# Weight halves in one ring of seven 8 KB tiles, and plain weights split two pairs at a time

## The chip, the cores and the metric

The kernel runs on one core of a Trainium2 chip. The metric is device time in microseconds (us): the time from start to end of one execution, the median of several. Before the change it is 1951.76 us, the median of three runs from 1951.52 to 1951.91.

A core has five engines, each with its own instruction stream: PE (TensorE, matrix products), DVE (VectorE, elementwise), ACT (ScalarE, elementwise and casts), POOL (GpSimd) and SP (SyncE, which here only issues transfers). They meet through semaphores. Transfers between the chip's memory and SBUF run on 16 DMA engines, which the queues of SP, ACT and POOL feed.

## The reference

One decoder block on 256 tokens of width 2048, all in float32. In short:

```python
h = x
h = h + 0.5 * swiglu(rms_norm(h, ffn1_norm), ffn1_w_gu, ffn1_w_down)    # FFN 1, inner width 5632
h = h + hybrid_mixer(rms_norm(h, mix_norm), w_in, ..., w_out)           # gated DeltaNet and stick-breaking heads
h = h + 0.5 * swiglu(rms_norm(h, ffn2_norm), ffn2_w_gu, ffn2_w_down)    # FFN 2
h = h + sigmoid(rms_norm(h, ple_norm) @ ple_w_gate) * (p @ ple_w_proj)
out = rms_norm(h, final_norm)

def swiglu(x, w_gu, w_down):
    gate, up = split(x @ w_gu, 2)
    return (silu(gate) * up) @ w_down
```

Nearly all the arithmetic is in the weight products. The two FFNs hold about two thirds of them.

## The kernel before

**Halves.** A float32 product is made from operands in a shorter type. Each operand is split: hi is the value cast to that type, lo is the rest, and a product is hi·hi + hi·lo + lo·hi: three matmuls of 128x512. For weights ACT makes hi (a cast, L74) and DVE makes lo (a subtract, L75). A *pair* is two 128-row slices of a block of 512 columns: 512 KB in memory, 4 KB in each of the 128 partitions. It is loaded to a raw tile by SP's queue (L71), split, and used by PE in 12 matmuls: two slices, two halves of the tokens, three products. `weight_pair` (L64 to 76) does this. There are four raw tiles, and three tiles each for hi and lo.

**Seven products.** In the FFNs part of the inner dimension is done by a Strassen-like scheme that makes seven products of eight. The four quarters of such a piece of weights (R0 to R3, 1 MB each, tag R) are loaded, DVE adds them up step by step (L304, some adds are done by an accumulating DMA on POOL's queue, L311), and at seven points the sum that then stands in a quarter is split to hi and lo (L295 on ACT, L296 on DVE; 128x2048 elements for a gate/up operand, 128x1536 or 128x1024 for a down product). `all_sums` is a generator for these seven operands, s0 to s6, with two tiles each for hi and lo of 8 KB. On the activations' side `halves` (L420 and on) builds the sums S and their halves Sh and Sl: an add (L452), four adds on quarters of it (L458), a cast (L460) and a subtract (L461). A full operand is used in 12 matmuls, one of a down product in 9 or 6. Each of the first four products is also copied or subtracted between banks (L344, L347, L349).

**Groups.** An FFN is a list of groups: 11 of gate/up (gu0 to gu10), each making 512 columns of gate and of up, and 6 of the down product (dn), two after each of the three parts of the inner dimension (3, 4 and 4 gate/up groups). The first or the second of two down groups makes columns 0 to 1023 or 1024 to 2047. While a group's plain pairs run, the seven products of the *next* group run between them, one after each plain pair from the second or third on. FFN 1 begins with two gate/up groups without seven-product operands, FFN 2 with one. At the end of a gate/up group DVE multiplies silu(gate) with up (L477), transposes it (L482) and later splits it (L500); after a down group's block DVE adds the result to h (L551).

**The order of the weights.** `plan` writes the whole order down ahead: a list of pairs, sum operands and loads of quarters. `next_weights` (L82 to 97) is called by PE's side for each operand that it uses. It goes through the list and issues what it may: pairs as long as no more than LEAD = 2 are split ahead of use, sum operands as long as no more than one is ahead. The two kinds are counted apart. A load in the list is issued when it is reached: the first four quarters of an FFN by SP's queue, the later ones by POOL's.

A scheduler then orders each engine's instructions by its own estimates. It keeps dependencies, and it may put matmuls of the hi half ahead of those of an operand whose lo half it expects late.

## Time and profile before

| | us |
|---|---|
| median of three runs | 1951.76 |
| the profiled run's own time | 1953.25 |
| its span in the profile | 1951.5 |
| granted TensorE clock, mean | 0.998 |
| PE / DVE / ACT busy | 1932.7 / 1567.9 / 1163.1 |
| DMA mean | 243 GB/s |

How to read the profile. The page gives busy time by engine and the chain of work that ended last, followed back from the last instruction. A group line gives the source line, engine, operation, the tile written and the tiles read, the shape, the number of instructions, then busy us and the mean ns of one, and behind the second bar the engine's idle time just ahead of them and what ended it. A timeline row has the start and the duration in us, the same names, and in brackets the idle time before it and what ended that; "x4" means four in a row put together. A row of the windows has, after the window and its length, the busy us of PE, PEld (weight loads, beside PE), DVE, ACT and POOL with the numbers of instructions, the granted clock, the busy share of the DMA engines and GB/s. SPq is SP's transfer queue.

### The profile page before, as it was taken

To read this page: it belongs to the slowest core of one execution; us is meant where nothing else is said; L and a number is where in the kernel's file an instruction comes from. 1 tells how busy PE (TensorE), PEld (TensorE's weight loads), DVE (VectorE), ACT (ScalarE), POOL (GpSimd) and SP (SyncE) were. 2 spreads that over 40 slices of the span, in tenths; PEclk is the share of its full clock that TensorE was granted. 3 is DMA by queue.
4 is the path that set the end of the run, shared out by engine and by line. 5 is a ranking of instruction groups with operands and counts; after the bars stand their busy time and mean duration, and the time that the engine had idled before them with its cause. 6 is when DMAs were issued, how large, how long until landed. Compare 5 with 4: busy or idle time off the path is not lost.

```text
span 1951.5 us, 24163 instructions
## 1 busy us (share of the span) xinstructions
PE 1932.7 (99%) x8884; PEld 1591.6 (82%) x8884; DVE 1567.9 (80%) x1679; ACT 1163.1 (60%) x1358; POOL 148.8 (8%) x226
## 2 busy tenths in 40 slices
PE   9999999999999999999999999999999999999997
PEld 7888888888888888878788888888888788887886
DVE  7889878997889766797856579889888987888965
ACT  6656666566665567664555456566565755656653
POOL 0010100000010000010100000010000100001000
PEclk9999999999999999999999999999999999999999
DMA  8778888788887765556565786888898987988864
GB/s 311 268 238 276 255 288 285 227 293 251 282 283 237 225 216 172 175 169 209 173 201 160 244 289 226 226 285 289 241 282 251 303 266 237 272 255 282 249 208 141
DMA packets 144184, 475.06 MB, mean 243 GB/s; under 512 B 19649, under 2 KB 47297, under 8 KB 129857
## 3 DMA queue, kind: packets, MB, share of 16 engines
q1 hardware_dynamic: 107200, 302.16, 44.4%
q0 software_dynamic: 25920, 160.44, 30.2%
q10 hardware_dynamic: 10944, 10.91, 1.7%
q8 instruction: 69, 1.13, 0.2%
q14 instruction: 51, 0.41, 0.1%
HBM read 451.44 MB, written 22.02 MB: 243 GB/s over the span
## 4 chain that ended last, share of the span: by engine, by line
PE 87%; DVE 6%; DMA 4%; issue 2%; ACT 1%; SPq 0%; POOL 0%; POOLq 0%; DVEq 0%; ACTq 0%
PE g L340 5%; PE d L541 5%; PE d L542 5%; PE g L339 5%; PE d L540 4%; PE g L341 4%; PE u L540 4%; PE u L542 4%; PE u L541 4%; PE g L541 4%; PE g L542 4%; PE pj L109 4%; PE pj L110 4%; PE pj L111 4%; PE g L540 4%
## 5 line engine op out<-in xcount | busy, mean ns | idle before, releaser
L74 ACT CAST whi<-raw 128x1024 fp32r<-128x1024 f32 (+1 forms) x489 | 512.1, 1050 | 427.1 <-PE pj L111 109.9
L75 DVE TENSOR_TENSOR wlo<-raw,whi 128x1024 fp32r<-128x1024 f32 (+1 forms) x489 | 592.0, 1217 | 166.1 <-ACT whi L74 163.8
L296 DVE TENSOR_TENSOR slo<-R,shi 128x2048 fp32r<-128x2048 f32 (+2 forms) x224 | 445.2, 1989 | 149.0 <-ACT shi L295 147.6
L295 ACT CAST shi<-R 128x2048 fp32r<-128x2048 f32 (+2 forms) x224 | 374.2, 1671 | 140.5 <-DVE R L304 62.1
L109 PE MATMUL pj<-whi,nTh 128*128 128x512 f32 x448 | 179.4, 401 | 0.0
L110 PE MATMUL pj<-wlo,nTh 128*128 128x512 f32 x448 | 175.3, 391 | 1.1 <-DVE wlo L75 1.1
L111 PE MATMUL pj<-whi,nTl 128*128 128x512 f32 x448 | 174.9, 390 | 0.0
L541 PE MATMUL d<-wlo,hTh 128*128 128x512 f32 x448 | 174.3, 389 | 0.0
L540 PE MATMUL d<-whi,hTh 128*128 128x512 f32 x448 | 174.2, 389 | 0.0
L542 PE MATMUL d<-whi,hTl 128*128 128x512 f32 x448 | 173.7, 389 | 0.0
L541 PE MATMUL g<-wlo,nTh 128*128 128x512 f32 x400 | 155.9, 390 | 0.4 <-DVE wlo L75 0.4
L541 PE MATMUL u<-wlo,nTh 128*128 128x512 f32 x400 | 155.7, 389 | 0.5 <-DVE wlo L75 0.5
L542 PE MATMUL g<-whi,nTl 128*128 128x512 f32 x400 | 155.8, 390 | 0.0
L542 PE MATMUL u<-whi,nTl 128*128 128x512 f32 x400 | 155.7, 389 | 0.0
L540 PE MATMUL g<-whi,nTh 128*128 128x512 f32 x400 | 155.4, 390 | 0.0
L540 PE MATMUL u<-whi,nTh 128*128 128x512 f32 x400 | 154.2, 389 | 0.2 <-ACT whi L74 0.2
L304 DVE TENSOR_TENSOR R<-R 128x2048 f32<-128x2048 f32 (+2 forms) x68 | 135.7, 1995 | 0.1
L110 PEld LDWEIGHTS pj<-wlo,nTh 128*128 128x128 f32 x448 | 84.2, 188 | 18.9 <-DVE wlo L75 2.7
L111 PEld LDWEIGHTS pj<-whi,nTl 128*128 128x128 f32 x448 | 84.1, 188 | 17.6
L542 PEld LDWEIGHTS d<-whi,hTl 128*128 128x128 f32 x448 | 84.1, 188 | 17.6
L541 PEld LDWEIGHTS d<-wlo,hTh 128*128 128x128 f32 x448 | 84.1, 188 | 17.6
L540 PEld LDWEIGHTS d<-whi,hTh 128*128 128x128 f32 x448 | 84.1, 188 | 17.4
(332 smaller groups left out, 3445.2 us busy)
## 6 DMA issues: line engine op xcount, KB each, us to landing
raw<-in_w_gu SPq DMA_DIRECT2D x199, 512.0 KB, 5.7
raw<-in_w_down SPq DMA_DIRECT2D x112, 512.0 KB, 6.5
raw<-in_w_in SPq DMA_DIRECT2D x112, 512.0 KB, 3.4
R<-in_w_gu2q POOLq DMA_DIRECT2D x54, 1024.0 KB, 8.6
R<-in_w_gu1q POOLq DMA_DIRECT2D x48, 1024.0 KB, 8.6
raw<-in_w_out SPq DMA_DIRECT2D x32, 512.0 KB, 4.2
tT<-scr SPq DMA_DIRECT2D x22, 512.0 KB, 5.1
R<-in_w_down11q POOLq DMA_DIRECT2D x12, 768.0 KB, 6.0
```

Of the source, the lines that this page charges most:

```text
L74: nc.scalar.copy(hi[:, j, :], raw[:, j, :])
L75: nc.vector.tensor_tensor(out=lo[:, j, :], in0=raw[:, j, :], in1=hi[:, j, :], op=ALU.subtract)
L109: nc.tensor.matmul(outs[t], xh[:, c], whi[:, j, :], start=st, stop=False)
L110: nc.tensor.matmul(outs[t], xh[:, c], wlo[:, j, :], start=False, stop=False)
L111: nc.tensor.matmul(outs[t], xl[:, c], whi[:, j, :], start=False, stop=sp)
L295: keep(nc.scalar.copy(hi, w))
L296: nc.vector.tensor_tensor(out=lo, in0=w, in1=hi, op=ALU.subtract)
L304: keep(nc.vector.tensor_tensor(out=self.raw[x], in0=self.raw[x], in1=self.raw[y], op=ALU.add))
L339: nc.tensor.matmul(out, xh, whi[:, g, :], start=st, stop=False, skip_group_check=True)
L540: nc.tensor.matmul(out, xh[:, c], whi[:, j, :], start=st, stop=False, skip_group_check=True)
L541: nc.tensor.matmul(out, xh[:, c], wlo[:, j, :], start=False, stop=False, skip_group_check=True)
L542: nc.tensor.matmul(out, xl[:, c], whi[:, j, :], start=False, stop=sp, skip_group_check=True)
```

## The change

It has three parts.

- **Raw tiles**: two of 8 KB in place of four of 4 KB. Each holds two pairs, loaded by two transfers, and is free again when both are split (class `Pairs`).
- **One ring.** The tiles for hi and lo of plain pairs (six of 4 KB) and of sum operands (four of 8 KB) become seven tiles of 8 KB: three in the pool that lives through the program (w), four in the FFN's (f), taken in the order of RING. A single pair takes one w tile for both halves. A sum operand, or a quad, takes two tiles, one for hi and one for lo. An operation is issued as soon as its tiles' last users are done in the list and not over `ahead` operations wait; that number doesn't bind, the seven tiles do.
- **Quads.** In the FFNs two plain pairs that follow one another in the list (other than the first two of an FFN, and those of FFN 2's last group) are split together: one cast and one subtract of 128x2048 (`halved`, L69 to 71). The lines are L70 (cast) and L71 (subtract) for plain weights, L392 and L393 for sum operands, L380 for the adds of quarters, L91 for the raw loads, L361 for the quarters, L569 and L574 for L477 and L482, L544, L550, L552 and L553 for S, and L644 for L551. Sum operands are made by `next_operand`, called once for each.

The built program has 154 quads, and 181 subtracts on plain weights that are not of a quad. The number of matmuls and their operands are unchanged, and the bytes loaded too.

The core of the diff:

```diff
-LEAD = 2
+RING = "ffwfwfw"
+CAP = {x: RING.count(x) for x in "wf"}
...
-        raw = wp.tile([P, 2, NB], F32, tag="raw", name="raw", bufs=4)
-        hi = pool.tile([P, 2, NB], F32R, tag="whi", name="whi", bufs=bufs)
-        lo = pool.tile([P, 2, NB], F32R, tag="wlo", name="wlo", bufs=bufs)
...
+    def new_raw():
+        return wp.tile([P, 4, NB], F32, tag="raw", name="raw", bufs=2)
+
+    def halved(hi, lo, src):
+        nc.scalar.copy(hi, src)
+        nc.vector.tensor_tensor(out=lo, in0=src, in1=hi, op=ALU.subtract)
...
+        def load(self):
+            if self.raw is None:
+                self.raw = new_raw()
+                n = 2 if done[0] else 1
+                for k in range(0, 2 * len(self.srcs), n):
+                    nc.sync.dma_start(out=self.raw[:, k:k + n], in_=self.srcs[k // 2][:, k % 2:k % 2 + n])
+            return self.raw
...
+        def issue(self, where):
+            slots = [(wp if x == "w" else current[0]).tile([P, NS, NB], F32R, tag="w", name="w",
+                                                            bufs=CAP[x]) for x in where]
+            if self.kind == "sum":
+                self.out = [self.src.next_operand(*slots)]
+            elif self.kind == "single":
+                raw = self.src.load()[:, 2 * self.at:2 * self.at + 2]
+                self.out = [weight_pair(raw, slots[0], 2 if not done[0] else 1)]
+            else:
+                halved(slots[0], slots[1], self.src.load())
+                self.out = [tuple(x[:, 2 * i:2 * i + 2] for x in slots) for i in range(2)]
...
     def next_weights():
 
-        ahead = max(1, min(LEAD, done[1] // 2))
-        while done[0] < len(order):
-            kind, src = order[done[0]]
-            if kind != "load" and sum(k == kind for k, _ in split) > (ahead if kind == "pair" else 1):
-                break
+        ahead = max(1, done[1] // 2)
...
+            if any(len(ring[x]) + where.count(x) - CAP[x] > sum(not o.left for o in ring[x][:where.count(x)])
+                   for x in "wf"):
+                break
+            if sum(o.left > 0 for o in set(ring["w"] + ring["f"])) > ahead:
+                break
+            op.issue(where)
...
-                hi = fp.tile([P, NS, NB], F32R, tag="shi", name="shi", bufs=2)[:, 0:self.ns]
-                lo = fp.tile([P, NS, NB], F32R, tag="slo", name="slo", bufs=2)[:, 0:self.ns]
...
+        pairs = [i for i in range(first, behind_at.get(n, len(order))) if order[i][0] == "pair"][2:]
+        quads.update(pairs[:len(pairs) // 2 * 2])
```

Two places where the built programs differ. The first is SP's queue at the end of the mixer and the start of FFN 2 (in_w_gu20 and in_w_gu2q are its first gate/up weights, plain and in quarters). Before:

```order
L71 DMA raw_9544<-in_w_gu20 128x1024
L71 DMA raw_9566<-in_w_gu20 128x1024
L71 DMA raw_9624<-in_w_gu20 128x1024
L71 DMA raw_9652<-in_w_gu20 128x1024
L71 DMA raw_9686<-in_w_gu20 128x1024
L71 DMA raw_9704<-in_w_gu20 128x1024
L276 DMA R_9658<-in_w_gu2q 128x2048
L276 DMA R_9660<-in_w_gu2q 128x2048
L276 DMA R_9662<-in_w_gu2q 128x2048
L276 DMA R_9664<-in_w_gu2q 128x2048
L71 DMA raw_9722<-in_w_gu20 128x1024
L71 DMA raw_9740<-in_w_gu20 128x1024
```

SP's queue at the same place, now:

```order
L91 DMA raw_8932<-in_w_gu20 128x1024 x2
L91 DMA raw_9010<-in_w_gu20 128x1024 x2
L361 DMA R_9015<-in_w_gu2q 128x2048
L361 DMA R_9017<-in_w_gu2q 128x2048
L361 DMA R_9019<-in_w_gu2q 128x2048
L361 DMA R_9021<-in_w_gu2q 128x2048
L91 DMA raw_9047<-in_w_gu20 128x1024 x2
L91 DMA raw_9074<-in_w_gu20 128x1024 x2
```

The loads of the fifth and sixth pair, raw_9686 and raw_9704 before, stood ahead of the four quarters; now (raw_9047) they stand behind them, where they wait for the subtract of the second pair.

The second place is DVE in FFN 1, in the second down group of the first part, while the products of the next gate/up group begin between its pairs (slo and w<-R are the lo halves of that group's operands s1 and s2, S its activations' sum, d0 and d1 the down product's banks). Before:

```order
L458 TENSOR_TENSOR S_1563<-S_1563 128x2x128
L75 TENSOR_TENSOR wlo_1573<-raw_1571,whi_1572 128x1024
L458 TENSOR_TENSOR S_1563<-S_1563 128x2x128
L75 TENSOR_TENSOR wlo_1613<-raw_1611,whi_1612 128x1024
L458 TENSOR_TENSOR S_1563<-S_1563 128x2x128
L296 TENSOR_TENSOR slo_1607<-R_1387,shi_1606 128x2048
L461 TENSOR_TENSOR Sl_1531<-S_1563,Sh_1530 128x1024
L551 SCALAR_TENSOR_TENSOR h_89<-d0_1307,h_89 128x512
L551 SCALAR_TENSOR_TENSOR h_89<-d1_1308,h_89 128x512
L75 TENSOR_TENSOR wlo_1650<-raw_1648,whi_1649 128x1024
L75 TENSOR_TENSOR wlo_1689<-raw_1687,whi_1688 128x1024
L296 TENSOR_TENSOR slo_1645<-R_1420,shi_1644 128x2048
```

DVE at the same place, now:

```order
L71 TENSOR_TENSOR w_1379<-raw_1380,w_1378 128x2048
L393 TENSOR_TENSOR w_1392<-R_1275,w_1391 128x2048
L544 TENSOR_TENSOR S_1431<-nTh_100,nTl_104 128x1024
L380 TENSOR_TENSOR R_1275<-R_1275,R_1323 128x2048
L550 TENSOR_TENSOR S_1431<-S_1431 128x2x128 x4
L393 TENSOR_TENSOR w_1440<-R_1275,w_1439 128x2048
L553 TENSOR_TENSOR Sl_1410<-S_1431,Sh_1409 128x1024
L380 TENSOR_TENSOR R_1275<-R_1275,R_1335 128x2048
L644 SCALAR_TENSOR_TENSOR h_89<-d0_1195,h_89 128x512
L644 SCALAR_TENSOR_TENSOR h_89<-d1_1196,h_89 128x512
L71 TENSOR_TENSOR w_1488<-raw_1489,w_1487 128x2048
L393 TENSOR_TENSOR w_1495<-R_1275,w_1494 128x2048
```

The narrow subtracts wlo_1573 and wlo_1613 stood among the adds of S, ahead of Sl and of the updates of h. The wide subtract of the quad w_1487 stands behind the second add of quarters (L380) and behind both updates of h (L644), and between it and the wide subtract of w_1378 there are twelve other instructions.

More of the change, by code (lines that the diff above doesn't have):

```diff
@@ L69, in weight_pair @@
+    def weight_pair(raw, w, parts=1):
         for i in range(parts):
             j = slice(2 * i // parts, 2 * (i + 1) // parts)
[L71 to L80 removed]
@@ L82, in next_weights @@
[L82 to L95 removed]
+            halved(w[:, 0:2][:, j], w[:, 2:4][:, j], raw[:, j])
@@ L399, in plan @@
             todo = []
+            if group.kind == "behind":
+                behind_at[n] = len(order)
             for j, (b, g) in enumerate(group.plain):
```

129 lines of the change are left out of this document (93 added, 36 removed).

## The prediction

> **What bounds the kernel now.** First the page: the span, the engines' busy time and the chain that ended last.
>
> ```profile
> span 1951.5 us, 24163 instructions
> PE 1932.7 (99%) x8884; PEld 1591.6 (82%) x8884; DVE 1567.9 (80%) x1679; ACT 1163.1 (60%) x1358; POOL 148.8 (8%) x226
> PE 87%; DVE 6%; DMA 4%; issue 2%; ACT 1%; SPq 0%; POOL 0%; POOLq 0%; DVEq 0%; ACTq 0%
> ```
>
> PE bounds it. The change leaves PE its 8884 matmuls, so its time is moved only by how long PE waits for operands. DVE and ACT have idle time of their own; what they save counts only where PE waits. The windows give each stage (first FFN, then the second; after the window come us and PE's busy time and instructions):
>
> ```profile
> 0.00:646.00 646.00, 642.84 (x2816) 527.05 (x2816) 546.11 (x480) 397.15 (x398) 57.35 (x92) 1.00 0.84 269
> 1155.40:1906.00 750.60, 748.77 (x3294) 614.29 (x3294) 636.83 (x568) 459.99 (x469) 64.32 (x98) 1.00 0.83 260
> ```
>
> A matmul is recorded longer than the distance to the next one, so a short wait hides between two records. I therefore count starts, in PE's timeline at the start of the second FFN:
>
> ```profile
> 1159.13 0.39 PE L540 MATMUL g<-whi,nTh 128*128 128x512 f32 x1
> ...
> 1167.29 0.39 PE L540 MATMUL g<-whi,nTh 128*128 128x512 f32 x1
> 1167.52 0.39 PE L541 MATMUL g<-wlo,nTh 128*128 128x512 f32 x1
> ```
>
> The first two rows are three pairs apart, 36 matmuls in 8.16 us: 0.2267 us each, 2.72 for a pair of weights (12 matmuls) and 2.72 for a full seven-product operand. At that pace the first FFN's 2816 matmuls take 638.4 of 646.0 us and the second's 3294 take 746.7 of 750.6. All waiting of PE in both FFNs is 7.6 + 3.9 = 11.5 us; no better feeding gains more there. The clock is 1.00 in both.
>
> How near to waiting PE already is shows in DVE's timeline where the first FFN goes from a down product back to gate/up, and in PE's beside it:
>
> ```profile
> 184.00 1.22 DVE L452 TENSOR_TENSOR S<-nTh,nTl 128x1024 f32<-128x1024 f32 x1
> 185.13 2.28 DVE L296 TENSOR_TENSOR slo<-R,shi 128x2048 fp32r<-128x2048 f32 x1
> 187.33 0.42 DVE L458 TENSOR_TENSOR S<-S 128x256 f32<-128x256 f32 x1
> 187.67 2.28 DVE L304 TENSOR_TENSOR R<-R 128x2048 f32<-128x2048 f32 x1
> 189.87 0.42 DVE L458 TENSOR_TENSOR S<-S 128x256 f32<-128x256 f32 x1
> ...
> 195.35 1.22 DVE L461 TENSOR_TENSOR Sl<-S,Sh 128x1024 fp32r<-128x1024 f32 x1
> 196.49 1.28 DVE L551 SCALAR_TENSOR_TENSOR h<-d,h 128x512 f32<-128x512 f32 x2
> 197.69 2.35 DVE L75 TENSOR_TENSOR wlo<-raw,whi 128x1024 fp32r<-128x1024 f32 x2
> 200.33 2.29 DVE L296 TENSOR_TENSOR slo<-R,shi 128x2048 fp32r<-128x2048 f32 x1 [0.29 <-ACT shi L295]
> ```
>
> ```profile
> 202.46 0.39 PE L339 MATMUL g<-shi,Sh 128*128 128x512 f32 x1
> 202.68 0.49 PE L340 MATMUL g<-slo,Sh 128*128 128x512 f32 x1
> ```
>
> The last low half is done at 200.33 + 2.29 = 202.62, and PE takes it at 202.68, 0.06 us later, and loses about 0.1. The slack at this place is nil. Whatever reaches DVE later than now is paid by PE in full.
>
> **The change, part by part.** The groups by form price its instructions (mean ns behind the busy time):
>
> ```profile
> L75 DVE TENSOR_TENSOR wlo<-raw,whi 128x1024 fp32r<-128x1024 f32 x487 | 590.6, 1219 | 164.5 <-ACT whi L74 162.2 <-DMA tT<-scr 1.5
> L296 DVE TENSOR_TENSOR slo<-R,shi 128x2048 fp32r<-128x2048 f32 x133 | 304.4, 2289 | 116.4 <-ACT shi L295 115.6 <-DMA raw<-in_w_gu 0.6
> L296 DVE TENSOR_TENSOR slo<-R,shi 128x1536 fp32r<-128x1536 f32 x56 | 98.2, 1755 | 22.7 <-ACT shi L295 22.3
> L304 DVE TENSOR_TENSOR R<-R 128x1536 f32<-128x1536 f32 x16 | 27.9, 1742 | 0.0
> ```
>
> ```profile
> L74 ACT CAST whi<-raw 128x1024 fp32r<-128x1024 f32 x487 | 510.8, 1052 | 425.6 <-PE pj L111 109.9 <-PE d L542 89.9 <-PE u L542 55.9
> L295 ACT CAST shi<-R 128x2048 fp32r<-128x2048 f32 x133 | 254.5, 1914 | 108.8 <-DVE R L304 53.7 <-PE g L341 31.0 <-PE u L341 18.3
> ```
>
> *One wide subtract and one wide cast for two pairs.* No row shows a wide one on plain weights; the sum operands' rows have the same shape and types, and I take those. DVE saves 2 x 1.219 - 2.289 = 0.149 us and ACT 2 x 1.052 - 1.914 = 0.190 on each of the program's 154 quads: 23 and 29 us of busy time. Both lie beside PE's work, so by themselves they are worth between 0 and the 11.5 above. What each quad pays is latency. From both raws landed to the first low half it is 1.914 + 2.289 = 4.2 us, where a single pair needs 1.052 + 1.219 = 2.27.
>
> A rule stands on each side of this. The Trainium skill, Perfetto Trace Analysis, section Optimizing Scalar/DVE Operations, gives DVE about 60 ns of overhead an instruction on SBUF and says that grouping helps if the engine is saturated; by that figure the 154 quads would save DVE an estimated 9 us, and the trace's 0.149 decides for 23. The same section says that where ScalarE and VectorE aren't saturated but cause bubbles elsewhere, breaking instructions up may let work finish sooner. At 80% and 60% busy this trace is the second case, and the change goes the other way.
>
> *One ring instead of two look-aheads.* Before, two pairs beyond the one in use and one sum operand beyond the one in use could be split at any time. Now a quad or a sum operand takes two of seven tiles: three such operations, and half a fourth, in use and ahead together. The quad's cast waits until PE has finished with the tiles of an operation three back.
>
> *The walk at one place: from a second down product to gate/up* (the DVE rows shown with the change). T = 0 is the first matmul of quad w_1369. PE then does its two pairs, half of w_1378, operand s0, the other half, s1, and after three high-half matmuls that the built program has in front it wants the low half of w_1487 after 75 matmuls: 75 x 0.2267 = 17.0. DVE: the cast of w_1378 waits for a tile last read just before T (-1.3) and ends at 0.6, its subtract starts at 0.65. Then, by the distances of starts in the timeline above, subtract 2.20, s0 2.20, S 1.13, R add 2.20: 8.4. s1's cast needs that add: 8.5 + 1.91, so s1's subtract starts at 10.45. Then 2.20, Sl 1.14, R add 2.20, two h updates 1.20: 17.2, and the quad's 2.29: 19.5. PE waits 2.5 us. The narrow subtracts that PE needs there today were made ahead of Sl and h. There are four such places, two in each FFN: **10 us**.
>
> *The other places by the same walk.* From gate/up into the first down product, DVE has behind the quad's predecessor two transposes, an R add (1.74), the S chain, s1's subtract (1.755), a second R add and Sl before the next quad's subtract; it comes 2.0 late: six places, **11**. Within first down products it is one R add fewer, 1.5: six places, **9**. From one gate/up group to the next, 0 to 1.2, taken 0.5: nine places, **4.5**. Each of these has 0 as its lower end, the slack seen today, and 4.2, a whole cast and subtract, as its upper.
>
> *The start of the second FFN.* Now six raws are queued ahead of the four R loads of 1 MB; with two raw tiles of two pairs there are four. SP's queue and ACT's casts, before:
>
> ```profile
> 1155.76 1.88 SPq L276 DMA_DIRECT2D R<-in_w_gu2q  x4
> 1158.74 21.54 SPq L71 DMA_DIRECT2D raw<-in_w_gu  x8
> ```
>
> ```profile
> 1171.17 1.06 ACT L74 CAST whi<-raw 128x1024 fp32r<-128x1024 f32 x1 [0.47 <-DMA raw<-in_w_gu]
> 1172.39 1.06 ACT L74 CAST whi<-raw 128x1024 fp32r<-128x1024 f32 x1 [0.16 <-DMA raw<-in_w_gu]
> ```
>
> The raw issued at 1158.74 lands only at 1171.1, behind the R loads. That is now the seventh; in the changed kernel the fifth and sixth stand there, issued behind the R loads when pair 1 is split (about 1158.7). Counted in bytes from the last raw before the R loads, sixth pair + R + seventh is now 5 MB by 1171.1, and R + fifth + sixth is 5 MB too. Their quad waits for both: cast from 1171.2, subtract from 1173.1, low half at 1175.4. PE wanted it at 1167.52 (row above): **8 us** (6.5 to 10 as the landing moves).
>
> *The start of the first FFN.* The quad of pairs 2 and 3 waits for both raws:
>
> ```profile
> 11.82 1.05 ACT L74 CAST whi<-raw 128x1024 fp32r<-128x1024 f32 x1 [0.30 <-DMA raw<-in_w_gu]
> ...
> 13.50 0.39 PE L541 MATMUL g<-wlo,nTh 128*128 128x512 f32 x1
> ```
>
> The second of them landed at 11.8. Cast 1.91 and subtract 2.29 end at 16.1; PE had the low half at 13.50: 2.6. With the first groups behind both starts, where quads meet the four R adds (1.7 each), **6**.
>
> *The mixer* keeps single pairs and three tiles. Raw tiles are freed two pairs at a time, which delays a load by 2.72 of the slack it has: 0, and at most a few us.
>
> Sum: 10 + 11 + 9 + 4.5 + 8 + 6 = 48.5, less the 11.5 of waits that these take the place of: +37. The profiled run took 1953.25, 1.5 above the median of the runs: 1953.25 + 37 - 1.5 = **1989 us**.
>
> **The rivals.** *The relief of DVE reaches PE* (0.13): 0.149 a quad brings every chain forward and the tiles suffice. The waits of 11.5 go, the DMA-bound 8 at the start stays: 1948; at best, with that covered too, 1940. For it speaks that DVE's chain ends at nil slack, so that each 0.1 counts. It decides if the chain walked above ends by 17.0 and not 19.5. It is what the Trainium skill's sentence on grouping (section named above) would make of this. Against it: the saving in that walk is two quads, 0.3 us.
>
> *Only the starts cost* (0.17): the scheduler's hoisted high halves cover the transitions, and 8 + 2.6 are left: about 1962.
>
> *One late operation holds all behind it* (0.12): tiles come back in the order of release, so lateness is not caught up in the long plain stretches. At 0.5 us for each of 154 quads it is 77: about 2027. It decides where a tile is released less than 4.2 us before its next use.
>
> *Nothing changes* (0.02): covers and losses cancel.
>
> **How the numbers follow.** The forecast has 0.56. A run of this kernel can tell about 0.2%, 3.9 us, from no change. The relief rival gives 0.08 to faster and 0.05 to same; with the last one that is 0.07. Slower: 0.56 + 0.17 + 0.12 = 0.85. The range leaves out most of the relief and most of the backlog: 1954 to 2018.
>
> **What would show it.** Right: matmuls still 0.2267 apart in the long plain stretches; at the start of the second FFN an 8 us hole on PE, ended by the wide subtract, whose cast is ended by a raw's landing; at each transition 1 to 3 us on PE, released by the wide subtract of plain weights with an R add, h or S ahead of it on DVE. The Trainium skill, Perfetto Trace Analysis, section Optimization Strategy, reads the same gap repeated on the engine that should be saturated as a possible want of tiles; no such gap is in today's trace. Wrong: PE's idle in either FFN below 2 us, a hole at the start under 4, or holes spread evenly over all quads.

## The result, and the profile after

After the change the kernel takes **2020.44 us** (median of four runs, 2018.13 to 2026.05) against 1951.67 for the kernel before beside it: a ratio of 1.0356, 95% interval 1.0335 to 1.0378. The forecast was slower, 1989, at most 2018. The sign was right, and so were the kinds of places where PE waits; the sum was 31 us short, and of what PE waits for at these places the forecast held about half.

The page of the changed kernel, with the span, busy times and the chain that ended last:

```profile
span 2016.4 us, 23675 instructions
PE 1954.8 (97%) x8884; PEld 1594.9 (79%) x8884; DVE 1562.1 (77%) x1525; ACT 1136.5 (56%) x1204; POOL 148.4 (7%) x226
PE 71%; DVE 12%; DMA 8%; ACT 4%; issue 3%; SPq 0%; ACTq 0%; POOL 0%; DVEq 0%; POOLq 0%
```

PE has the same 8884 matmuls. DVE has 154 instructions fewer, yet its share of the chain that ended last doubles from 6 to 12%, and DMA's from 4 to 8%: DVE is a little less busy, and PE waits more for it and for transfers. The subtracts on plain weights, in the groups by line:

```profile
L71 DVE TENSOR_TENSOR w<-raw,w 128x1024 fp32r<-128x1024 f32 (+2 forms) x335 | 571.7, 1709 | 252.6 <-ACT w L70 174.0
```

All subtracts on plain weights together were 592.0 us and are 571.7: 20 saved in this row, where 23 was forecast. DVE as a whole saved only 5.8 us (1567.9 to 1562.1). The records of instructions that follow one another directly overlap: two narrow subtracts take 2.35 together, so the second starts 1.13 behind the first, and a wide one is followed 2.20 behind its start (both in the prediction's rows). Where they stand back to back, a quad thus saves 2 x 1.13 - 2.20 = 0.06, not 0.149. The saving is small and buys nothing.

**The start of the second FFN.** PE's timeline, before and behind its two longest waits, then ACT's and DVE's:

```profile
1199.27 0.39 PE L635 MATMUL g<-w,nTl 128*128 128x512 f32 x1
1205.36 1.22 PE L633 MATMUL g<-w,nTh 128*128 128x512 f32 x2 [5.71 <-ACT w L70]
1207.69 0.80 PE L634 MATMUL g<-w,nTh 128*128 128x512 f32 x1 [1.10 <-DVE w L71]
1208.28 0.63 PE L635 MATMUL g<-w,nTl 128*128 128x512 f32 x1
1208.70 0.63 PE L634 MATMUL g<-w,nTh 128*128 128x512 f32 x1
```

```profile
1203.41 1.90 ACT L70 CAST w<-raw 128x2048 fp32r<-128x2048 f32 x1 [1.54 <-DMA raw<-in_w_gu]
1205.83 1.91 ACT L70 CAST w<-raw 128x2048 fp32r<-128x2048 f32 x1 [0.52 <-DMA raw<-in_w_gu]
```

```profile
1205.34 4.72 DVE L71 TENSOR_TENSOR w<-raw,w 128x2048 fp32r<-128x2048 f32 x2 [2.21 <-ACT w L70]
```

The wide subtract's cast (1203.41) was ended by a raw's landing, as forecast. PE's waits beyond the 0.2267 pitch are 5.9 and 1.5 us, 7.4 together (forecast 8). The last two rows show something that the forecast lacked: matmuls recorded 0.63 long and about 0.43 apart. The window over this place shows why (clock 0.50 behind the busy times):

```profile
1205.30:1210.00 4.70, 3.54 (x8) 2.35 (x9) 4.53 (x2) 1.91 (x2) 0.00 (x0) 0.50 0.29 92
```

**The place that was walked** (second down product to gate/up, first part of the first FFN), DVE, ACT and PE:

```profile
203.58 2.29 DVE L393 TENSOR_TENSOR w<-R,w 128x2048 fp32r<-128x2048 f32 x1 [0.31 <-ACT w L392]
205.79 1.22 DVE L553 TENSOR_TENSOR Sl<-S,Sh 128x1024 fp32r<-128x1024 f32 x1
206.92 2.28 DVE L380 TENSOR_TENSOR R<-R 128x2048 f32<-128x2048 f32 x1
209.12 1.28 DVE L644 SCALAR_TENSOR_TENSOR h<-d,h 128x512 f32<-128x512 f32 x2
210.32 2.28 DVE L71 TENSOR_TENSOR w<-raw,w 128x2048 fp32r<-128x2048 f32 x1
```

```profile
209.29 1.90 ACT L392 CAST w<-R 128x2048 fp32r<-128x2048 f32 x1 [2.48 <-DVE R L380]
```

```profile
211.25 0.79 PE L418 MATMUL g<-w,Sh 128*128 128x512 f32 x1 [2.04 <-ACT w L392]
212.66 0.79 PE L634 MATMUL d<-w,hTh 128*128 128x512 f32 x1 [0.62 <-DVE w L71]
```

The wide subtract stands behind Sl, the R add and both h, and PE takes its result at 212.66, 0.06 us after its end at 212.60. That wait is 1.2 us. The longer one ahead of it, 2.2 us, isn't for the quad: a seven-product matmul (L418) takes an operand's high half at 211.25, and that operand's cast stood idle for 2.48 us until the R add (206.92 to 209.20) was done. Behind both waits comes again a stretch of matmuls recorded 0.63 long.

**From gate/up into the first down product** (gu6 to dn1a, first FFN), DVE, with PE's wait behind it:

```profile
368.11 1.71 DVE L380 TENSOR_TENSOR R<-R 128x1536 f32<-128x1536 f32 x1
...
371.74 1.34 DVE L550 TENSOR_TENSOR S<-S 128x256 f32<-128x256 f32 x3
373.00 1.75 DVE L393 TENSOR_TENSOR w<-R,w 128x1536 fp32r<-128x1536 f32 x1
...
375.01 1.75 DVE L380 TENSOR_TENSOR R<-R 128x1536 f32<-128x1536 f32 x1
376.68 1.22 DVE L553 TENSOR_TENSOR Sl<-S,Sh 128x1024 fp32r<-128x1024 f32 x1
...
378.42 2.28 DVE L71 TENSOR_TENSOR w<-raw,w 128x2048 fp32r<-128x2048 f32 x1
```

```profile
380.75 0.50 PE L634 MATMUL u<-w,nTh 128*128 128x512 f32 x1 [1.61 <-DVE w L71]
```

```profile
369.48 1.92 ACT L70 CAST w<-raw 128x2048 fp32r<-128x2048 f32 x1 [6.67 <-PE g L634]
```

This quad's cast ends at 371.40, and its subtract begins 7.0 us later, behind an operand's subtract, an R add, Sl and parts of the S chain that the scheduler put first. It is an order of DVE's queue, not a transfer, that PE waits for here. The cast itself was held until PE gave a tile back (the bracket of the last row).

**Where the time went.** A wait is counted as the distance of two starts of PE beyond 0.2267 us; "slow" is what matmuls lose that run 0.43 apart behind it. Before, the two FFNs had 12.8 us of waits (the prediction took 11.5) and none slow.

| place | forecast, gross | waits after | slow after |
|---|---|---|---|
| start of the second FFN (gu0) | 8 | 9.6 | 1.9 |
| start of the first FFN (gu0, gu1) | 6 | 7.9 | 1.8 |
| second down product to gate/up, four places | 10 | 10.4 | 2.6 |
| gate/up into and within first down products | 20 | 31.3 | 1.4 |
| gate/up to gate/up | 4.5 | 10.1 | 0 |
| all | 48.5 | 69.3 | 7.7 |

69.3 + 7.7 - 12.8 = 64.2 of the spans' difference of 64.9 (2016.4 - 1951.5); the mixer and the end make the rest. The gate/up groups gu3, gu4, gu7 and gu8 of both FFNs wait for at most 0.1 us each.

**Gate/up to gate/up** isn't 0.5 at each of nine places: it is 2.4 to 2.5 at four (gu5 and gu9 of both FFNs) and nothing at the rest. ACT at one of the four, and the late subtract on DVE:

```profile
333.78 1.91 ACT L392 CAST w<-R 128x2048 fp32r<-128x2048 f32 x1 [1.65 <-DVE R L380]
...
337.31 0.57 ACT L423 COPY u<-u 128x512 f32<-128x512 f32 x1 [1.03 <-PE u L420]
...
338.37 1.91 ACT L70 CAST w<-raw 128x2048 fp32r<-128x2048 f32 x1
```

```profile
340.31 2.29 DVE L71 TENSOR_TENSOR w<-raw,w 128x2048 fp32r<-128x2048 f32 x1 [2.29 <-ACT w L70]
```

The quad's cast stands behind the next operand's cast (333.78), which waits for an R add, behind a copy that waits for PE, and an activation (337.79). DVE has idled 2.29 us when it comes.

### The profile page after: what moved, and what is told of

Its sections match the earlier page's. It is cut to its first block, busy times and chain, and to the rows that moved or that the text cites. A ratio compares the mean times of both kernels' runs of the same rounds, so it can differ in the third digit from the quotient of the medians.

```text
span 2016.4 us, 23675 instructions
## 1 busy us (share of the span) xinstructions
PE 1954.8 (97%) x8884; PEld 1594.9 (79%) x8884; DVE 1562.1 (77%) x1525; ACT 1136.5 (56%) x1204; POOL 148.4 (7%) x226
## 3 DMA queue, kind: packets, MB, share of 16 engines
q8 instruction: 69, 1.13, 0.2%
## 4 chain that ended last, share of the span: by engine, by line
PE 71%; DVE 12%; DMA 8%; ACT 4%; issue 3%; SPq 0%; ACTq 0%; POOL 0%; DVEq 0%; POOLq 0%
DVE w L71 5%; PE pj L194 4%; PE pj L195 4%; PE pj L196 4%; PE g L418 4%; PE g L419 4%; PE u L634 4%; PE g L420 4%; PE u L635 4%; PE u L633 3%; PE g L634 3%; DMA raw<-in_w_gu 3%; PE g L635 3%; PE g L633 3%; PE d L634 3%
## 5 line engine op out<-in xcount | busy, mean ns | idle before, releaser
L71 DVE TENSOR_TENSOR w<-raw,w 128x1024 fp32r<-128x1024 f32 (+2 forms) x335 | 571.7, 1709 | 252.6 <-ACT w L70 174.0
L70 ACT CAST w<-raw 128x1024 fp32r<-128x1024 f32 (+2 forms) x335 | 483.1, 1444 | 354.3 <-PE pj L196 102.8
L392 ACT CAST w<-R 128x2048 fp32r<-128x2048 f32 (+2 forms) x224 | 372.5, 1671 | 301.1 <-DVE R L380 187.7
L393 DVE TENSOR_TENSOR w<-R,w 128x2048 fp32r<-128x2048 f32 (+2 forms) x224 | 443.4, 1986 | 123.0 <-ACT w L392 88.9
L634 PE MATMUL d<-w,hTh 128*128 128x512 f32 x448 | 176.9, 395 | 3.0 <-DVE w L71 2.9
L194 PE MATMUL pj<-w,nTh 128*128 128x512 f32 x448 | 179.7, 401 | 0.0
L195 PE MATMUL pj<-w,nTh 128*128 128x512 f32 x448 | 175.3, 391 | 1.1 <-DVE w L71 1.1
L635 PE MATMUL d<-w,hTl 128*128 128x512 f32 x448 | 175.1, 392 | 0.0
L196 PE MATMUL pj<-w,nTl 128*128 128x512 f32 x448 | 174.9, 390 | 0.0
L633 PE MATMUL d<-w,hTh 128*128 128x512 f32 x448 | 173.2, 392 | 0.0
L634 PE MATMUL u<-w,nTh 128*128 128x512 f32 x400 | 157.0, 393 | 8.8 <-DVE w L71 8.8
L633 PE MATMUL g<-w,nTh 128*128 128x512 f32 x400 | 156.9, 395 | 7.3 <-ACT w L70 7.3
L634 PE MATMUL g<-w,nTh 128*128 128x512 f32 x400 | 157.7, 394 | 2.8 <-DVE w L71 2.5
L633 PE MATMUL u<-w,nTh 128*128 128x512 f32 x400 | 153.0, 390 | 1.3 <-ACT w L70 1.3
L380 DVE TENSOR_TENSOR R<-R 128x2048 f32<-128x2048 f32 (+2 forms) x68 | 136.1, 2001 | 0.7
```

The source lines that it names most:

```text
L70: nc.scalar.copy(hi, src)
L71: nc.vector.tensor_tensor(out=lo, in0=src, in1=hi, op=ALU.subtract)
L194: nc.tensor.matmul(outs[t], xh[:, c], whi[:, j, :], start=st, stop=False)
L195: nc.tensor.matmul(outs[t], xh[:, c], wlo[:, j, :], start=False, stop=False)
L196: nc.tensor.matmul(outs[t], xl[:, c], whi[:, j, :], start=False, stop=sp)
L380: keep(nc.vector.tensor_tensor(out=self.raw[x], in0=self.raw[x], in1=self.raw[y], op=ALU.add))
```

## The experiments

Each kernel was timed in three rounds beside the kernel before; its ratio to that has its 95% interval behind it. "FFN 2 start" is the length of the second FFN's first group on PE: 64.7 us before, 75.4 after.

### What each part does in the changed kernel

**Narrow instructions.** The quad keeps its tiles and its raw tile, but each of its pairs has a cast and a subtract of its own:

```diff
-                halved(slots[0], slots[1], self.src.load())
+                raw = self.src.load()
+                for i in (slice(0, 2), slice(2, 4)):
+                    halved(slots[0][:, i], slots[1][:, i], raw[:, i])
```

> The changed kernel with each quad split by two narrow casts and two narrow subtracts (128x1024) into the same two tiles of the ring; raw tiles, ring and order of the weights stay. If the waits come from the width of one cast and one subtract (4.2 us from raw to the first low half, against 2.3), then the first low half comes 1.9 us earlier at each of some 20 places that now wait 1 to 3 us, most of these waits go, the clock's drops behind them too, and the time falls to about 1980. If they come from the seven tiles (a quad can start only when an operation three back is done), the start of each split is where it was, DVE has 23 us more to do, and the time stays at 2010 to 2028.

Measured: 1990.27, 1.020 (1.0183 to 1.0217). The width is worth 30 of the 69 us; 39 remain with instructions as narrow as before's.

**One of the two wide.** First one wide cast and two narrow subtracts; then two narrow casts and one wide subtract:

```diff
-                halved(slots[0], slots[1], self.src.load())
+                nc.scalar.copy(slots[0], raw)
+                for i in (slice(0, 2), slice(2, 4)):
+                    nc.vector.tensor_tensor(out=slots[1][:, i], in0=raw[:, i], in1=slots[0][:, i], op=ALU.subtract)
```

> The changed kernel with one wide cast but two narrow subtracts for each quad. Narrow casts and subtracts gave 1990, wide ones 2020. If the time follows the latency to the first low half (2.27, here 1.91 + 1.22 = 3.1, 4.2), this one lies in between, 2000 to 2006. If only the wide subtract hurts, by keeping DVE from what is queued behind it, 1988 to 1994. If only the wide cast hurts, by ACT's queue, 2014 to 2022.

```diff
-                halved(slots[0], slots[1], self.src.load())
+                for i in (slice(0, 2), slice(2, 4)):
+                    nc.scalar.copy(slots[0][:, i], raw[:, i])
+                nc.vector.tensor_tensor(out=slots[1], in0=raw, in1=slots[0], op=ALU.subtract)
```

> The changed kernel with two narrow casts and one wide subtract for each quad. With one wide cast and two narrow subtracts it took 2002, with both wide 2020, with none 1990. If the time follows the latency to the first low half, 2 x 1.05 + 2.29 = 4.4 us is as late as with both wide: 2016 to 2026. If the wide cast costs by itself on ACT's queue what the other run gained, 2006 to 2012.

Measured: 2001.60, 1.0256 (1.024 to 1.0271), and 2027.82, 1.0383 (1.0367 to 1.0399). The second saves as many instructions on DVE as the change does and is no faster than it (the intervals of the two overlap). The order of the four is that of the time from the landed raw to the first low half: 1.05 + 1.22 = 2.3 us (1990), 1.91 + 1.22 = 3.1 (2002), 1.91 + 2.29 = 4.2 (2020), 2 x 1.05 + 2.29 = 4.4 (2028). By their ratios these are 20, 26, 36 and 38 thousandths. So the cost of the width goes with latency, some 13 to 18 us for each us of it; the number of instructions shows no effect. A wide cast costs 11 us where the subtracts are narrow and nothing where the subtract is wide, so it isn't the length of ACT's instructions as such. Whether a wide subtract also costs by keeping DVE from what is queued behind it, these four can't tell.

**The ring without quads**, raw tiles still of two pairs:

```diff
-        quads.update(pairs[:len(pairs) // 2 * 2])
+        quads.update(pairs[:0])
```

> The changed kernel without quads: every plain pair is split by itself into one tile, the sum operands and the pairs share the ring of seven, raw tiles hold two pairs. If width is the cause, only the raw loads behind the quarters at the start of the second FFN are left, where a single pair is ready about 3 us sooner than a quad: about 5 us, so 1955 to 1962. If sharing seven tiles is the cause, most of the loss stays: 1985 or more.

Measured: 1997.59, 1.0235 (1.022 to 1.0251). Single pairs in the ring are no better than quads with narrow instructions. It isn't quite the same ring, since a single pair takes a w tile only and a sum operand takes any; that quads as such cost nothing is shown below, by the kernel of 1953 us.

**The raw tiles alone**: no quads, and the sum operands have their four f tiles to themselves again, the pairs the three w tiles.

```diff
-        return "".join(RING[(done[2] + i) % len(RING)] for i in range(2))
+        return "ff"
...
-        quads.update(pairs[:len(pairs) // 2 * 2])
+        quads.update(pairs[:0])
```

> As the run without quads, but the sum operands take only the four tiles of the FFN's pool and the pairs only the other three, as in the kernel before: what is left of the change are the raw tiles of two pairs each. Both theories: the start of the second FFN alone, about 5 us, 1955 to 1960. At 1970 or more, raw tiles that come free two pairs at a time cost more than the start, and both theories are short of a cause.

Measured: 1982.67, 1.0157 (1.0141 to 1.0172). Far more than the start of the second FFN (71.6, +7). The rest are holes of 3.5 to 3.9 us at the ends of gu6 and gu10 of both FFNs. At the first of them, one row each of SP's queue, of POOL's accumulating transfer, and of ACT and PE behind them:

```profile
361.78 3.70 SPq L91 DMA_DIRECT2D raw<-in_w_down  x4
```

```profile
360.71 0.88 POOL L387 DMA_DIRECT2D R<-in_w_down11q  x1 [13.25 <-DVE S L550]
```

```profile
369.35 1.04 ACT L70 CAST w<-raw 128x1024 fp32r<-128x1024 f32 x1 [4.07 <-DMA raw<-in_w_down]
```

```profile
372.82 0.56 PE L418 MATMUL d<-w,Sh 128*128 128x512 f32 x1 [3.78 <-ACT part L426]
```

In the kernel before the same raws are issued one by one, from ahead of the accumulating transfer on. SP's queue and POOL's:

```profile
355.04 10.31 SPq L71 DMA_DIRECT2D raw<-in_w_down  x5
```

```profile
358.22 0.88 POOL L311 DMA_DIRECT2D R<-in_w_down11q  x1 [12.27 <-DVE S L458]
```

A raw tile of two pairs is free only when both are split, so here the load is issued 1.1 us behind a transfer of 768 KB (a quarter of this down product; a quarter of gate/up is 1 MB) and not 3.2 ahead of it, lands 7.5 us after its issue (4.2 before), and ACT waits 4.07 for it.

**The same without the accumulating transfers** (the quarters are then not added up there, so that part of the sums is left out):

```diff
-                nc.gpsimd.dma_start(out=self.raw[x], in_=self.quarters[y[1]][y[0]], accum_op=ALU.add)
+                pass
```

> The run with only the raw tiles changed, without the accumulating transfers of quarters on POOL's queue (that part of the sums is left out). In that run PE waits 3.5 to 3.9 us in gate/up groups 6 and 10 for a raw load that was issued at 361.8 and landed at 369.2, behind a 1 MB accumulating transfer issued at 360.7. If the raw load is late because it falls behind that transfer, the four holes go, with the slow clock behind them: about 20 us less, 1962. If it is late because it is issued late, when both pairs of its tile are split, they stay: 1978 to 1983.

Measured: 1957.64, 1.0029 (1.0018 to 1.004). The four holes go (gu6 of the first FFN 42.5 to 36.9 us) and with them 25 us. So those transfers are what the late raws run into; whether their bytes or their place in time weigh more, a kernel without them can't tell. What stays is the start of the second FFN (72.1).

**Four raw tiles of one pair**, first with the quads narrow, then without quads:

```diff
-        return wp.tile([P, 4, NB], F32, tag="raw", name="raw", bufs=2)
+        return wp.tile([P, 2, NB], F32, tag="raw", name="raw", bufs=4)
...
+                raws = [self.src.load(i) for i in range(2)]
+                for i, raw in enumerate(raws):
+                    j = slice(2 * i, 2 * i + 2)
+                    halved(slots[0][:, j], slots[1][:, j], raw)
```

> The run with narrow casts and subtracts in quads, and four raw tiles of one pair each in place of two of two: a raw tile is free for the next load when its own pair is split. The first batch gave raw tiles of two pairs 31 us when all else was as before. If they cost that whatever the ring does, this run comes to 1959 to 1966. If their loss is the same waiting that ring and quads cause anyway, it stays at 1980 or more.

> The run without quads in the ring of seven, with four raw tiles of one pair each: the ring alone is left of the change. If the three parts add up, 1998 less 31 is 1967, 15 us above the kernel before, with the waits where sum operands and pairs compete for tiles. If the ring costs nothing by itself, 1952 to 1955; if raw tiles were not the cause in the ring, 1985 or more.

Measured: 1986.19, 1.0177 (1.0162 to 1.0192), and 1992.39, 1.0203 (1.0186 to 1.022). The start of the second FFN is mended (66.2 and 66.8), but in all only 4 to 5 us come back. So raw tiles alone cost 31 and the ring alone costs 40, and both together 46: a pair that is late for a tile loses nothing more when its raw is late too (argued, not shown). The longest rows of what the ring alone makes of PE's waits:

```profile
PE d L637 <- DVE w L71: 7.6, 11, 1.5
PE u L636 <- ACT w L70: 6.3, 12, 1.0
```

(Total, times, longest.) Mostly not a few holes but many, of a fraction of a us up to 1.5, for low and high halves of plain weights.

**The first quarters two pairs later** in the list:

```diff
-                    loads.setdefault(max(at[0] - 5, 0), []).extend(follower.loads())
+                    loads.setdefault(max(at[0] - 3, 0), []).extend(follower.loads())
```

> The changed kernel with the first four quarters of each FFN put two pairs later in the list of weights, so that in the second FFN the raw loads of pairs 5 and 6 stand ahead of the four quarters. If the hole at the start (5.9 + 1.5 us of waiting and the slow clock behind it) comes from that order of loads, it goes: 8 to 11 us less, about 2010. If the hole comes from the ring or from the quad's width alone, the time stays at 2020.

Measured: 2018.04, 1.0339 (1.0324 to 1.0355). The FFN 2 start is 72.3: the hole keeps its cause but moves two pairs on, to waits of 2.9 and 1.8 us between 1201 and 1207. With two raw tiles some raw still stands behind the quarters.

### An eighth tile

The eighth tile needs 8 KB. All kernels of this section take them from the low halves of the hidden activations (hTl), in whose place the down products read the high halves again; the matmuls stay as many. The first kernel is the control, with seven tiles:

```diff
+                        tl = fp.tile([P, 4, T], F32R, tag="hTl", name="hTl", bufs=2)
...
-                        hTl.append(tl)
+                        hTl.append(th)
```

> The changed kernel, with the low halves of the FFNs' hidden activations still made but not read (the matmuls and the sums on them read the high halves in their place), which gives up 8 KB a partition. It is the control for the runs with eight tiles: PE, DVE and ACT have the same work, so 2014 to 2026.

```diff
-RING = "ffwfwfw"
+RING = "ffwffwfw"
```

> As the control, with an eighth tile of 8 KB for the ring (five in the FFN's pool): four operations in use and ahead in place of three and a half. If the ring's cost is that an operation can start only when a tile comes free, the places lose one to two us each: 1985 to 2005. If the cost is the chain from sum to cast to subtract to PE on engines that work in order, whatever tiles are free, 2012 or more.

Measured: control 2022.07, 1.035 (1.0335 to 1.0366), the change's own time; with eight tiles 1998.72, 1.0229 (1.0206 to 1.0253). The seventh-to-eighth step is worth 23 us. The four waits at gu5 and gu9 vanish. ACT at the place shown above:

```profile
333.09 1.92 ACT L70 CAST w<-raw 128x2048 fp32r<-128x2048 f32 x1
...
338.43 3.72 ACT L392 CAST w<-R 128x2048 fp32r<-128x2048 f32 x2
```

The quad's cast (333.09) now stands ahead of an operand's, and nothing waits.

**Eight tiles with the edits shown above**: narrow instructions; then four raw tiles as well; then, with these, no quads.

```diff
+                for i in (slice(0, 2), slice(2, 4)):
+                    halved(slots[0][:, i], slots[1][:, i], raw[:, i])
...
+        return wp.tile([P, 2, NB], F32, tag="raw", name="raw", bufs=4)
...
+        quads.update(pairs[:0])
```

> Eight tiles (low halves of the hidden activations not read, as in the control) and two narrow casts and subtracts for each quad. With seven tiles this took 1990. If tiles are what the ring lacks, 1962 to 1975, and what is left is the raw loads. If not, 1982 or more.

> Eight tiles, narrow splits (low halves of the hidden activations not read, as in the control) and four raw tiles of one pair each in place of two of two. That leaves the ring with quads held over two pairs as the only change. If the raw tiles cause what eight tiles left, 1983 falls to 1968 or less, with the start of the second FFN near 66 us as in the other runs with four raw tiles. If it is DVE's order, where narrow subtracts still stand behind adds of quarters, it stays at 1975 or more.

> Eight tiles, four raw tiles (low halves of the hidden activations not read), no quads, the ring shared by pairs and sum operands. With seven tiles this took 1992, with waits of 1 to 3 us at most transitions. If the pairing makes what is left, 1955 to 1965. If the sharing does, 1975 or more, and an eighth tile that only one operation in two can use helps little.

Measured: 1983.54, 1.0162 (1.0145 to 1.0179); 1982.38, 1.0159 (1.0144 to 1.0174); 2004.55, 1.0265 (1.025 to 1.028). With eight tiles, narrow instructions and four raw tiles, 31 us are still there, and without quads it is worse than with seven tiles (1992). Neither width, raws nor the number of tiles is this rest.

**Eight tiles, not shared.** The same eight, but the sums keep four of their own and the quads take turns in three w tiles and one other. Narrow, four raw tiles:

```diff
-        return "".join(RING[(done[2] + i) % len(RING)] for i in range(2))
+        if op.kind == "sum":
+            return "ff"
+        return ("ww", "wq")[done[2] % 2]
```

> Eight tiles, narrow splits, four raw tiles (low halves of the hidden activations not read), with no sharing: sum operands use four tiles of the FFN's pool, quads the three others and one of their own. Only that two pairs are issued and held as one is left of the change. If the sharing makes what is left, 1955 to 1965. If the pairing does, 1975 or more.

Measured: 1953.23, 1.0009 (0.9999 to 1.0018). All of the loss is gone, quads and all. Its page:

```profile
span 1951.5 us, 24035 instructions
PE 1930.6 (99%) x8884; PEld 1593.1 (82%) x8884; DVE 1564.9 (80%) x1679; ACT 1150.5 (59%) x1358; POOL 148.4 (8%) x226
```

**From there back, one part at a time:** two raw tiles of two pairs; then the wide cast and subtract too.

```diff
-        return wp.tile([P, 2, NB], F32, tag="raw", name="raw", bufs=4)
+        return wp.tile([P, 4, NB], F32, tag="raw", name="raw", bufs=2)
...
+                halved(slots[0], slots[1], self.src.load())
```

> As the run of 1953 us (eight tiles, sums and quads on tiles of their own, narrow splits, low halves of the hidden activations not read), but with two raw tiles of two pairs each. In the kernel before, with pairs one by one, they cost 31 us: at the start of the second FFN and at four places in gate/up groups 6 and 10. If that doesn't depend on the rest, 1975 to 1990. If the pairing, which loads two pairs at a time anyway, takes that cost away, 1953 to 1965.

> As that, with one wide cast and one wide subtract for each quad as well: the whole change but for the sharing of tiles, with one tile more. In the ring of seven the wide instructions cost 30 us, in the ring of eight 15. If they cost because the ring leaves too little time ahead, they cost less than 6 us above the run with raw tiles of two pairs here. If two pairs' latency counts by itself, 15 or more above it.

Measured: 1963.28, 1.0062 (1.0045 to 1.0079), and 1973.62, 1.0112 (1.0091 to 1.0134). The longest wait of the first is the forecast one, for a raw at the start of the second FFN:

```profile
PE g L637 <- ACT w L69: 4.1, 1, 4.1
```

The chain of five kernels is then:

| kernel | us | step |
|---|---|---|
| eight tiles apart, narrow, four raw tiles | 1953 | |
| + raw tiles of two pairs | 1963 | 10 |
| + wide cast and subtract | 1974 | 10 |
| + one ring for pairs and sums | 1999 | 25 |
| + seven tiles instead of eight (control) | 2022 | 23 |

The two largest steps are both the ring. By the ratios to the kernel before, the step of 25 is 23; with narrow instructions and four raw tiles sharing costs 29 (1953 to 1982). The step of 10 for the wide instructions lies between the two bounds set for it (under 6, or 15 and more) and decides for neither. No kernel of the study beat the kernel before; the first equals it, with 8 KB more for the ring and the low halves left unread.

### The slow matmuls

The changed kernel, with 30 matmuls of 128x512 into a bank that nothing reads, put into PE's stream just ahead of the fifth pair of the second FFN, to fill its wait:

```diff
+                    if n == "2" and group is ffn_plan[n][0][0] and (b, g) == (0, 4):
+                        idle = mx_ps("idle")
+                        for _ in range(30):
+                            tc.keep_in_program_order(nc.tensor.matmul(
...
```

> The changed kernel with 30 matmuls of 128x512 on activations, into a bank that nobody reads, ahead of the fifth pair of the second FFN, where PE pauses 5.9 and 1.5 us for the raw loads. They take 6.8 us. If the half pace behind that pause (8 matmuls, 1.9 us) comes from PE standing idle, it goes: matmuls 0.227 apart from the first, granted clock 1.00 in the 10 us behind the pause, the group 2 us shorter, 2018. If it comes from the stage (its transfers, or what DVE does then), it stays and the fillers run at half pace too or the matmuls behind them do.

Measured: 2017.55, 1.0339 (1.0321 to 1.0356). PE there, and the window:

```profile
1201.57 6.96 PE L628 MATMUL idle<-nTh 128*128 128x512 f32 x30
1209.94 0.50 PE L640 MATMUL g<-w,nTh 128*128 128x512 f32 x1 [0.95 <-DVE w L71]
1210.28 0.40 PE L641 MATMUL g<-w,nTl 128*128 128x512 f32 x1
```

```profile
1205.00:1210.00 5.00, 4.04 (x19) 3.04 (x17) 2.50 (x2) 3.81 (x2) 0.00 (x0) 1.00 0.23 94
```

The clock is 1.00 and the matmuls behind are 0.40 long, not 0.63. The group shrinks from 75.4 to 74.0. PE's own pause makes it slow, not the late operand. In the whole time the 1.4 us are within the intervals.

## Why the prediction was right and wrong

**Right: the sign, and the start of the second FFN.** Two of the three marks that it gave show: the hole at the start of the second FFN, with the landing behind it, and nothing in the long plain stretches. The hole was forecast at 8 and is 7.4, or 9.6 with the other waits of its group. The relief rival fails: of the kernels with seven tiles the one with narrow casts and wide subtracts saves DVE as much and is no faster than the change. The Trainium skill, Perfetto Trace Analysis, section Optimizing Scalar/DVE Operations, says that where ScalarE and VectorE aren't saturated, breaking instructions up may let work finish sooner. The runs agree: 30 us between wide and narrow. The price of that relief was misread too: 0.149 a quad came from records that overlap, and DVE's busy time fell by 5.8 us, nearer to the 9 that the prediction set aside than to its 23.

**Wrong: what PE waits for besides.** This is the step that failed. The sum had prices for the low halves of quads alone. An operand of the seven products, with its R add, its cast and its subtract, and the copies between banks that queue with the casts on ACT, were in no term. In the changed kernel's list of PE's waits (total, times, longest) the longest row for plain weights and the longest for an operand are:

```profile
PE u L634 <- DVE w L71: 8.8, 11, 1.6
PE g L418 <- ACT w L392: 5.1, 5, 2.0
```

All rows of that list for matmuls of the FFNs on plain weights come to 22.8 us, and those for seven-product matmuls to 23.4. In the kernel before, the two are 1.1 and 3.0.

**Right in size by luck: the four walked transitions** (10; 10.4). The third mark, 1 to 3 us at each, released by the wide subtract of plain weights, shows at one of the four: there it ended 1.2 us, and at the other three nothing. Operands' casts ended 5.2 of the 10.4 (2.2 at the walked place, 0.9, 1.1 and 1.0 at two others), operands' low halves 1.6. The four are 4.1, 1.0, 2.2 and 3.1, where the walk has 2.5 for each.

**Wrong: "The other places by the same walk".** Two terms, taken from slack instead of walked. Gate/up into and within first down products was 20 and is 31.3. The DVE rows at 368 to 378 have the R adds, the S chain, the operand's subtract and Sl that the text listed, ahead of the quad's subtract; but PE waits in down products for more than that subtract. Rows of the same list for tiles of the down products:

```profile
PE d L418 <- ACT part L426: 4.1, 4, 3.0
PE d L418 <- ACT w L392: 3.7, 2, 3.0
PE d L418 <- ACT Sh L552: 3.3, 3, 2.3
PE d L634 <- DVE w L71: 2.9, 7, 0.8
```

The term priced waits like the last row and the one at 380.75. The three rows above it, 11.1 us, are seven-product matmuls that wait for ACT: for a copy between banks, an operand's cast, an activations' cast. (The first row has four waits in the kernel before too, 2.7 us.) The longest of the first row, on PE, and ACT ahead of it:

```profile
174.74 0.50 PE L418 MATMUL d<-w,Sh 128*128 128x512 f32 x1 [2.95 <-ACT part L426]
```

```profile
173.16 1.04 ACT L392 CAST w<-R 128x1024 fp32r<-128x1024 f32 x1 [2.58 <-DMA R<-in_w_down10q]
```

The copy stands behind an operand's cast that waits 2.58 us for an accumulating transfer. The longest of the second row, at 1351.3, is the same cast in the second FFN, 2.60 us. So the two longest waits in down products, 6.3 us of PE's time, go back to a transfer: those of 512 KB landed 9.5 and 9.6 us after their issue, and 5.8 and 5.6 in the kernel before. What delays them was not tried. Gate/up to gate/up was 0.5 at each of nine and is 2.5 at four: there a cast on ACT, not DVE's row, came late. That is 17 of the 28.5 us by which the gross sum was short. (The rest of the 31 lies in which runs are compared: the profiled run of after, 2018.13, is 2.3 below its median, that of before was 1.5 above.)

**Missing: the clock behind a wait.** Half pace was in no term: 7.7 us. The trace of before has no such stretch.

**Too low: the start of the first FFN**, 6 against 7.9. (The credit for before's own waits was too low as well, 11.5 against 12.8, which goes the other way.)

**The rival "one late operation holds all behind it"** gave 2027, the nearest number, by a mechanism that doesn't show: its 0.5 us for each quad would show in gu3, gu4, gu7 and gu8, which have none. Its time is near by chance.

**What the text named too lightly: the ring.** It told of the tile that must come back, and let the price come from latency and from one walk. The chain shows latency at 10 us when tiles are ample, 30 when they are not. Sharing costs 25 more at the same number of tiles, and the eighth tile gives 23. In the shared order a pair's tile is given back by a sum operand's last product and the reverse, so a pair can be held by an operand that itself waits for an R add. That is argued; shown is the price of sharing as a whole, eight shared against eight apart. How the 25 divide between tiles that come back late and an order of ACT and DVE that the scheduler chose is open, and no order written by hand was tried. That the order has a part is seen in the kernel with eight shared tiles and narrow instructions, where narrow subtracts still stand behind an R add on DVE, 2.7 us after their casts end at 196.53, and PE waits 1.6 us for them:

```profile
197.07 2.28 DVE L382 TENSOR_TENSOR R<-R 128x2048 f32<-128x2048 f32 x1
199.27 2.35 DVE L71 TENSOR_TENSOR w<-raw,w 128x1024 fp32r<-128x1024 f32 x2
```

## What to carry to other kernels

Where one engine is 99% busy, ask of an edit on the others how late its first result comes, not how many instructions it saves: here one wide instruction instead of two cost 10 to 30 us while both engines that it relieved had idle time. Two streams of operands that are used in turn but made at different speeds should keep buffers of their own; at equal bytes, sharing cost 23 to 29 us of 1953. And a buffer that holds two loads is refilled at the pace of the later: look which large transfer gets ahead of it.

## What the runs showed of the hardware

**Half pace behind a wait.** In the twenty traces there are 58 stretches in which PE's matmuls of 128x512 come 0.427 us apart instead of 0.2267, recorded 0.63 instead of 0.39, with a granted clock of 0.50 where a window holds nothing else. They last 3 to 13 such steps, most often 7, which loses 1.4 us (13 lose 2.6). Every wait of over 3.2 us was followed by one; of the waits of 2.1 to 3.1 us some were (one of 3.11 was not); of single waits under 1.77 none, but two shorter ones close together could be (1.3 and 1.2 us in the kernel with the 30 extra matmuls). The Trainium skill, TensorE: Matmul & The Clock Gate, section What's actually happening, says that the clock halves after an idle window of about 3.4 us and that the window runs freely. The trace agrees above 3.2 us and with the varying outcome, but shows half pace behind shorter waits too. A wait of over 2 us on PE is thus to be priced at up to 2.6 us more than its length, most often at 1.4 or at nothing.

**A raw load of 512 KB** landed 4.2 us after its issue where it was issued 3.2 us ahead of an accumulating transfer of 768 KB of another queue, and 7.5 us where it was issued 1.1 us behind it. In the kernel before, the next raw was issued 1.1 us behind that transfer too, and landed 7.7 us after its issue. These are single loads, not means.
